# Group norms of a state-space head: token sums and the root's spread moved from TensorE to VectorE's 32x32 transposes and five small transfers

## The chip, the cores and the metric

The kernel runs on one core of a Trainium2 chip. The metric is the device time of one execution in microseconds (us). A core has five engines that work side by side, each through its own list of instructions in a fixed order: TensorE (PE; its weight loads are shown as PEld), VectorE (DVE), ScalarE (ACT), GpSimd (POOL) and SyncE (SP), which here only issues transfers (DMAs). An instruction waits for others by semaphores, and all behind it on its engine wait with it.

## What is computed

One step of a hybrid decoder layer in float32, for 320 tokens: 256 of a prompt and 8 sequences of 8 new ones. The part that matters is the end of the state-space head (SSD). Its output has 2048 columns in four groups of 512; each group has a root-mean-square norm of its own:

```
y = y.reshape(bsz, L, SSM_WIDTH) * jax.nn.silu(z.astype(f32))
yg = y.reshape(bsz, L, SSM_GROUPS, SSM_WIDTH // SSM_GROUPS)
yg = yg * lax.rsqrt(jnp.mean(yg * yg, axis=-1, keepdims=True) + EPS)
y = yg.reshape(bsz, L, SSM_WIDTH) * norm_w.astype(f32)
```

So for every token and group 512 squares are summed, and a root of the mean scales the group. Then `mix = concat(gate_out, y) @ w_out`, a norm and a residual, and a feed-forward part.

## The kernel before, in words

**Layout.** Activations are kept with columns on the 128 partitions and the 320 tokens along the free axis; a group is four blocks of 128x320 (tile `xs`, called y). A sum over a group's columns is therefore one over partitions. Device time goes mostly into products with the weights. Each weight slab of 128x1024 (512 KB) is issued by SP (L118), rounded to a high part on ScalarE (`whi`, L124), and its low part is made on VectorE (`wlo`, L125). Three products (L153 to L155) take the parts with the high and low parts of the activations. Raw, high and low slabs have three buffers each. SP issues a slab when the subtraction three slabs earlier has freed its buffer; ScalarE casts a slab when TensorE has freed the high part three slabs earlier.

**Order.** The program is emitted in a hand-written order: the products of a projection, with small background tasks taken from a list `bg`, one step at each `tick()`, usually one or two per slab. Each engine's list follows from that order and from priorities (`first()` moves things ahead). The SSD of group g (`ssd`) and its norm are such tasks. `heads_out(g, ...)` (L1027) projects z; its evacuation `z_evac` gates y and adds the squares of the four blocks on VectorE to `ssq` (128x320: a partition's sum over four blocks). The task `norm` (L1042) then waits `later` steps (2 or 3), sums and takes the root, waits as many steps, spreads the root, and multiplies and splits y into `ohi`/`olo` (for group 3 into the last blocks of `h_hi`/`h_lo`). These are read by `chunk_out(w_out, 4 + g, ...)` (L1063 to L1080), products `pd` that VectorE adds to `acc_mix` (L249). Between norm and chunk lies the projection of the next group's x (`heads_in_next`), for groups 0 and 1; the chunk of one group overlaps the SSD of the next one.

**The norm.** `token_sums` (L291) has TensorE multiply three slices of `ssq` by a column of ones, giving the 320 sums as three columns over the tokens' partitions. `rsqrt_of` (L258) makes the root on VectorE in eleven small steps on 128x3. `spread` (L300) brings it back to all partitions by three transposes of a broadcast column on TensorE, into PSUM, where the multiplication (L1051) reads it.

**Around it.** In the SSD, cumulative sums come from device memory (`cs<-dacs_d`, L816), become decays on ScalarE (L969, L970) and are masked on VectorE (L972); TensorE reads them for `y_ps` (L983). `xsp` (L842) is the low part of a product operand for `up_ps` (L904). `load_x` (L1110) issues loads of x (`xr`) on SP, used after chunk 7.

Of the kernel before, what the change touches and what calls it, by code (L numbers as in the profile page):

```python
# [9 lines left out]
F32 = mybir.dt.float32  # L10
# [3 lines left out]
ALU = mybir.AluOpType  # L14
# [3 lines left out]
P = 128  # L18
# [3 lines left out]
NT = NP + NS  # L22
# [12 lines left out]
def hybrid_step(  # L35
# [10 lines left out]
    act, dve, pool, pe, sp = nc.scalar, nc.vector, nc.gpsimd, nc.tensor, nc.sync  # L46
# [4 lines left out]
    dr = ctx.enter_context(tc.tile_pool(name="dr", bufs=1, space=DRAM))  # L51
    wp = ctx.enter_context(tc.tile_pool(name="wp", bufs=3))
    tp = ctx.enter_context(tc.tile_pool(name="tp", bufs=2))
# [3 lines left out]
    def misc(name):  # L57
        return ms.tile([P, 512], F32, tag="ms", name=name)
# [41 lines left out]
    def col(i):  # L100
        return prm[:, i:i + 1]


    def first():

        return tc.high_priority(offset=200000)
# [66 lines left out]
    def finish(task):  # L173
        while task in bg:
            tick()
# [79 lines left out]
        pd_last.append(made)  # L255


    def rsqrt_of(ss, scale, n, rows=P):  # L258

        v = tp.tile([P, n], F32, tag=f"rs_v{n}", name="rs_v")[:rows]  # L260
        r = tp.tile([P, n], F32, tag=f"rs_r{n}", name="rs_r", bufs=3)[:rows]
        t = tp.tile([P, n], F32, tag=f"rs_t{n}", name="rs_t")[:rows]
        dve.tensor_scalar(out=v, in0=ss, scalar1=scale, scalar2=EPS, op0=ALU.mult, op1=ALU.add)
        dve.tensor_scalar(out=r.bitcast(I32), in0=v.bitcast(I32), scalar1=-0.5, scalar2=float(0x5F3759DF),
                          op0=ALU.mult, op1=ALU.add)
        for _ in range(3):
            dve.scalar_tensor_tensor(out=t, in0=v, scalar=-0.5, in1=r, op0=ALU.mult, op1=ALU.mult)
            dve.tensor_tensor(out=t, in0=t, in1=r, op=ALU.mult)
            ins = dve.scalar_tensor_tensor(out=r, in0=t, scalar=1.5, in1=r, op0=ALU.add, op1=ALU.mult).ins
        rsqrt_ins.append(ins)  # L270
        return r
# [3 lines left out]
    def rsqrt_by_root(rest, ps, scale, rows=P):  # L275

        v = tp.tile([P, 3], F32, tag="rs_v3", name="rs_v")[:rows]
        r = tp.tile([P, 3], F32, tag="rs_r3", name="rs_r", bufs=3)[:rows]
        t = tp.tile([P, 3], F32, tag="rs_t3", name="rs_t")[:rows]
        s = tp.tile([P, 3], F32, tag="rs_s3", name="rs_s")[:rows]  # L280
        dve.tensor_scalar(out=v, in0=ps if rest is None else rest, scalar1=scale, scalar2=EPS, op0=ALU.mult, op1=ALU.add)
        if rest is not None:
            dve.scalar_tensor_tensor(out=v, in0=ps, scalar=scale, in1=v, op0=ALU.mult, op1=ALU.add)
        rooted.append(act.activation(s, v, AF.Sqrt).ins)
        dve.reciprocal(r, s)
        dve.scalar_tensor_tensor(out=t, in0=v, scalar=-0.5, in1=r, op0=ALU.mult, op1=ALU.mult)
        dve.tensor_tensor(out=t, in0=t, in1=r, op=ALU.mult)
        rsqrt_ins.append(dve.scalar_tensor_tensor(out=r, in0=t, scalar=1.5, in1=r, op0=ALU.add, op1=ALU.mult).ins)
        return r

    def token_sums(*sqs):  # L291

        ps = misc("tsum")
        for c, o in enumerate((0, P, NT - P)):
            for i, sq in enumerate(sqs):
                ins = pe.matmul(ps[:, c:c + 1], sq[:, o:o + P], ones[:, 0:1], start=i == 0, stop=i == len(sqs) - 1).ins  # L296
        sums_ins.append(ins)
        return ps[:, 0:3]

    def spread(r, out=None):  # L300

        ps = misc("spread")
        for c, o in ((2, NT - P), (0, 0), (1, P)):
            spread_ins.append(pe.transpose(ps[:, o:o + P], r[:, c:c + 1].to_broadcast([P, P]), ident).ins)
        if out is not None:
            act.copy(out, ps[:, :NT])
        return ps[:, :NT]

    def add_square(total, x, begins, adder=pool, place=("sq", 2)):
        if begins:  # L310
            act.activation(total, x, AF.Square)
        else:
            sq = tp.tile([P, NT], F32, tag=place[0], name="sq", bufs=place[1])
            act.activation(sq, x, AF.Square)
            adder.tensor_tensor(out=total, in0=total, in1=sq, op=ALU.add)
# [23 lines left out]

    dacs_d = dr.tile([NH, NT + NS], F32, name="dacs_d")  # L340
    tot_d = dr.tile([NH, NB], F32, name="tot_d")


    hp = ctx.enter_context(tc.tile_pool(name="hp", bufs=1))
# [22 lines left out]
    def scaled(ps, func, out):  # L367

        ev = tp.tile([P, NT], F32, tag="pv", name="ev", bufs=4)
        with first():  # L370
            dve.tensor_tensor(out=ev, in0=ps[:, :NT], in1=r1, op=ALU.mult)
        func_ins.append(act.activation(out, ev, func).ins)

    def split(hi, lo, x, scale=None):

        if scale is None:
            act.copy(hi, x)
            made = dve.tensor_tensor(out=lo, in0=x, in1=hi.bitcast(F32), op=ALU.subtract)
        else:
            act.activation(hi, x, AF.Copy, scale=scale)  # L380
            made = dve.scalar_tensor_tensor(out=lo, in0=x, scalar=scale, in1=hi.bitcast(F32), op0=ALU.mult, op1=ALU.subtract)

        return made.ins

    def out_parts(pool_, name):
        return (pool_.tile([P, 4, NT], F32R, tag=f"{name}hi", name=f"{name}hi"),
                pool_.tile([P, 4, NT], F32R, tag=f"{name}lo", name=f"{name}lo"))
# [12 lines left out]
    with ExitStack() as mctx:  # L400
        op = mctx.enter_context(tc.tile_pool(name="op", bufs=1))
# [153 lines left out]
        with tc.tile_pool(name="gp", bufs=1) as gp:  # L555
# [44 lines left out]
            def root():  # L600

                dve.tensor_tensor(out=acc[:, 0, :], in0=acc[:, 0, :], in1=acc[:, 1, :], op=ALU.add)
                ps = misc("tsum")
                for c in range(2):
                    pe.matmul(ps[:, c:c + 1], acc[:, 0, P * c:P * c + P], ones[:, 0:1], start=True, stop=True)
                for h in range(2):
                    pe.matmul(ps[64 * h:64 * h + 64, 2:3], acc[:, 0, NP:NT], ones[:, 0:1], start=True, stop=True, tile_position=(0, 64 * h))
                return rsqrt_of(ps[:, 0:3], 1.0 / D, 3)
# [7 lines left out]
            for n in range(2):  # L616
                ps = banks("ps_v")
                for kt in range(KD):
# [16 lines left out]
                    if n == 0 and kt == 12:  # L635
                        r = root()
# [22 lines left out]
                with first():  # L659
                    for c, g in ((0, 0), (0, 1), (1, 0), (1, 1), (2, 0), (2, 1)):  # L660
                        at, src = slice(0, NS if c == 2 else P), ps[c][g]
                        if c == 2:
# [4 lines left out]
                                                       scale=r[at, c:c + 1]).ins)  # L667
# [4 lines left out]
            def layer_norm():  # L672
# [3 lines left out]
                for c, (o, n) in enumerate(TOK):  # L676
# [3 lines left out]
                    dve.bn_aggr(mv[:n, c, :], st[:n].rearrange("p a b -> p (a b)"))  # L680
                    yield
                lr = rsqrt_of(mv[:, :, 1], 1.0, 3)
                rows = []

# [82 lines left out]
        with tc.tile_pool(name="sd", bufs=1) as sd:  # L767
# [7 lines left out]
            for c in range(4):  # L775
# [6 lines left out]
                else:  # L782
                    b = bsp[:, c - 2]
# [243 lines left out]
            def heads_out(g, rate, later):  # L1027

                ssq = hp.tile([P, NT], F32, tag="ssq", name="ssq")
                y = x_of.pop(g)  # L1030

                def z_evac(j, ps):
                    if j == 0:
                        finish(tasks[g])
                    zs = tp.tile([P, NT], F32, tag="ev", name="zs", bufs=2)
                    with first():
                        scaled(ps, AF.Silu, zs)
                        dve.tensor_tensor(out=y[:, j, :], in0=y[:, j, :], in1=zs, op=ALU.mult)
                        add_square(ssq, y[:, j, :], j == 0, dve)
                project(w_in, Z0 + 512 * g, z_evac, quiet=4, rate=rate)  # L1040

                def norm():  # L1042
                    yield from repeat(None, later)
                    with first():
                        r = rsqrt_of(token_sums(ssq), 1.0 / 512, 3)
                    yield from repeat(None, later)
                    rb = spread(r)

                    res[g] += [h[:, KD - 4:] for h in hT] if g == 3 else out_parts(hp, "o")
                    for j in range(4):  # L1050
                        dve.tensor_tensor(out=y[:, j, :], in0=y[:, j, :], in1=rb, op=ALU.mult)  # L1051
                        split(res[g][0][:, j, :], res[g][1][:, j, :], y[:, j, :], col(prm_at["norm"][3] + 4 * g + j))
                task = norm()
                bg.insert(0, task)
                return task
# [30 lines left out]
            with first():  # L1086
# [8 lines left out]
                r = rsqrt_by_root(most, ps, 1.0 / D)  # L1095
# [48 lines left out]
    with tc.tile_pool(name="fp", bufs=1) as fp:  # L1144
# [149 lines left out]
        r = rsqrt_by_root(most, ps, 1.0 / D)  # L1294
# [7 lines left out]
        for k in BY_POOL:  # L1302
            f = acc[:, k, :]
# [111 lines left out]
```

## Time and profile before

| | |
|---|---|
| median of 3 runs | 1779.38 us (1778.97 to 1780.19) |
| span of the profiled execution | 1779.7 us |
| busy: PE, PEld, VectorE, ScalarE, GpSimd | 99, 96, 66, 46, 15% |
| granted TensorE clock | 0.999 of full |
| moved by DMA | 289.91 MB, 163 GB/s |
| sums of the four groups' squares on TensorE (L296) | 24 records, from 541.8 to 774.8 us |

How to read it: the span runs from the first instruction to the last of one execution with the profiler on, and stands for that execution's own time; it lies 0.3 us above the median of the timed runs and between their ends. Busy shares are averages over stages. A matmul's record is longer than the distance to the next one, since matmuls are pipelined; their starts show the pace. "A <- B: 3.4, 4, 0.9" in a list of waits means that A stood 3.4 us in all for B, 4 times, 0.9 at most. A group row has count, busy us and mean ns, then the idle time just before. A row of DMA issues ends with the median time from issue to landing. In a timeline row stand start, length, engine, line, operation, out<-in, and in brackets the idle time before it and what ended it.

### The profile page before, as it was taken

The numbers are of one execution on the slowest core, as the hardware profiler recorded it, in microseconds if no ns is written. First come the engines' busy times: TensorE is split into PE (matmuls) and PEld (weight loads), VectorE is DVE, ScalarE is ACT, GpSimd is POOL, SyncE is SP. The second block draws the span as 40 slices with busy tenths as digits, with TensorE's granted clock in tenths as the row PEclk, the third lists the DMA queues.
The fourth block names the chain that finished last, engine by engine and source line by source line (L and its number), as shares of the span: only waits on it lengthen the run. The fifth ranks groups of instructions, "written<-read, shape, count | busy, mean of one in ns | idle before, by whom it ended". The sixth has DMA issues, their size and how long they took to land.

```text
span 1779.7 us, 30655 instructions
## 1 busy us (share of the span) xinstructions
PE 1770.5 (99%) x11933; PEld 1715.7 (96%) x11933; DVE 1168.0 (66%) x1999; ACT 819.5 (46%) x1195; POOL 273.5 (15%) x602
## 2 busy tenths in 40 slices
PE   9999999999999999999999999999999999999998
PEld 7789999999999998999999999999999999999998
DVE  7549764656977768677865464756656575656575
ACT  5434555334564547445545333343434343433445
POOL 1202200000331313103121011110102020101004
PEclk9999999999999999999999999999999999999999
DMA  7546645456665665554554545545545545454543
GB/s 260 163 148 177 189 128 154 153 153 188 216 190 190 181 207 168 168 171 145 180 156 146 157 149 151 155 148 152 157 144 156 150 150 155 150 150 155 147 154 107
DMA packets 214417, 289.91 MB, mean 163 GB/s; under 512 B 16384, under 2 KB 143744, under 8 KB 214080
## 3 DMA queue, kind: packets, MB, share of 16 engines
q1 hardware_dynamic: 202544, 268.74, 49.6%
q10 hardware_dynamic: 10016, 14.16, 2.2%
q0 software_dynamic: 1712, 5.05, 1.0%
q8 instruction: 94, 1.54, 0.4%
q14 instruction: 51, 0.42, 0.1%
HBM read 273.08 MB, written 14.82 MB: 162 GB/s over the span
## 4 chain that ended last, share of the span: by engine, by line
PE 97%; DVE 1%; ACT 0%; DMA 0%; issue 0%; POOL 0%; POOLq 0%; ACTq 0%; DVEq 0%
PE ps L153 19%; PE ps L155 19%; PE ps L154 19%; PE pd L153 10%; PE pd L155 10%; PE pd L154 10%; PE ps_v L144 7%; PE y_ps L983 1%; PE up_ps L904 0%; PE yo_ps L887 0%; PE sg L731 0%; PE xt_ps L393 0%; DMA cs<-dacs_d 0%; PE x1p L1278 0%; PE tsum L296 0%
## 5 line engine op out<-in xcount | busy, mean ns | idle before, releaser
L125 DVE TENSOR_TENSOR wlo<-wraw,whi 128x1024 fp32r<-128x1024 f32 (+1 forms) x476 | 582.5, 1224 | 432.4 <-ACT whi L124 430.1
L124 ACT CAST whi<-wraw 128x1024 fp32r<-128x1024 f32 (+1 forms) x475 | 494.8, 1042 | 729.9 <-PE ps L154 392.1
L153 PE MATMUL ps<-h_hi,whi 128*128 128x320 f32 x2268 | 704.0, 311 | 0.0
L154 PE MATMUL ps<-h_lo,whi 128*128 128x320 f32 x2268 | 702.7, 310 | 0.0
L155 PE MATMUL ps<-h_hi,wlo 128*128 128x320 f32 x2268 | 702.2, 310 | 0.0
L153 PEld LDWEIGHTS ps<-h_hi,whi 128*128 128x128 f32 x2268 | 426.2, 188 | 2.6 <-issue 1.6
L154 PEld LDWEIGHTS ps<-h_lo,whi 128*128 128x128 f32 x2268 | 426.3, 188 | 0.7
L155 PEld LDWEIGHTS ps<-h_hi,wlo 128*128 128x128 f32 x2268 | 426.2, 188 | 0.0
L155 PE MATMUL pd<-fhi,wlo 128*128 128x320 f32 x704 | 218.2, 310 | 0.0
L153 PE MATMUL pd<-fhi,whi 128*128 128x320 f32 x704 | 218.2, 310 | 0.0
L154 PE MATMUL pd<-flo,whi 128*128 128x320 f32 x704 | 218.2, 310 | 0.0
L153 PE MATMUL pd<-ohi,whi 128*128 128x320 f32 x448 | 139.4, 311 | 0.0
L155 PE MATMUL pd<-ohi,wlo 128*128 128x320 f32 x448 | 138.7, 310 | 0.0
L154 PE MATMUL pd<-olo,whi 128*128 128x320 f32 x448 | 138.7, 310 | 0.0
L153 PEld LDWEIGHTS pd<-fhi,whi 128*128 128x128 f32 x704 | 132.1, 188 | 0.0
L154 PEld LDWEIGHTS pd<-flo,whi 128*128 128x128 f32 x704 | 132.1, 188 | 0.0
L155 PEld LDWEIGHTS pd<-fhi,wlo 128*128 128x128 f32 x704 | 132.1, 188 | 0.0
L1180 POOL COPY ptf<-pad 128x2 f32<-128x2 f32 x88 | 21.0, 239 | 603.7 <-DVE pad L1168 603.0
L249 DVE TENSOR_TENSOR acc_ffn<-acc_ffn,pd 128x320 f32<-128x320 f32 (+1 forms) x161 | 77.5, 482 | 37.8 <-PE pd L155 36.5
L153 PEld LDWEIGHTS pd<-ohi,whi 128*128 128x128 f32 x448 | 84.1, 188 | 1.4 <-issue 1.0
L154 PEld LDWEIGHTS pd<-olo,whi 128*128 128x128 f32 x448 | 84.1, 188 | 0.3
L155 PEld LDWEIGHTS pd<-ohi,wlo 128*128 128x128 f32 x448 | 84.1, 188 | 0.1
(328 smaller groups left out, 1867.9 us busy)
## 6 DMA issues: line engine op xcount, KB each, us to landing
wraw<-in_ffn_w_up SPq DMA_DIRECT2D x176, 512.0 KB, 3.7
wraw<-in_w_in SPq DMA_DIRECT2D x140, 512.0 KB, 3.8
wraw<-in_ffn_w_down SPq DMA_DIRECT2D x88, 512.0 KB, 3.4
wraw<-in_w_out SPq DMA_DIRECT2D x64, 512.0 KB, 3.4
st<-in_state_ssm SPq DMA_DIRECT2D x32, 256.0 KB, 3.9
out_ssm_state_sample<-st ACTq DMA_DIRECT2D x30, 256.0 KB, 3.4
cs<-dacs_d SPq DMA_DIRECT2D x16, 320.0 KB, 4.7
xr<-in_xT SPq DMA_DIRECT2D x4, 640.0 KB, 4.0
```

The lines of the kernel that those rows point to most:

```text
L124: rounded[:] = [act.copy(hi, raw).ins]
L125: dve.tensor_tensor(out=lo, in0=raw, in1=hi.bitcast(F32), op=ALU.subtract)
L144: made = pe.matmul(out, xi, w[g][wi], start=first and begins, stop=last and ends)
L153: pe.matmul(ps, whi, xhi, start=first, stop=False)
L154: pe.matmul(ps, whi, xlo, start=False, stop=False)
L155: return pe.matmul(ps, wlo, xhi, start=False, stop=last).ins
L249: added_last[:] = [dve.tensor_tensor(out=acc[:, nb, ts], in0=acc[:, nb, ts], in1=ps[:, ts], op=ALU.add).ins]
L983: pe.matmul(ps[64 * i:64 * i + 64, cols], w(hl), x(hl, m, cpx), tile_position=(0, 64 * i), **flags)
L1180: pool.tensor_copy(ptf[:, k, :], pad[:, 256:258])
```

## The change

The sums of the four group norms and the spread of their root no longer use TensorE. `partial_sums` transposes `ssq` in blocks of 32x32 on VectorE, so that a partition holds 32 partitions' values of ten tokens; a sum along the free axis leaves 128x10: for each of four bands of 32 partitions the partial sums of 320 tokens. SP stores these 5 KB to device memory, and four loads (32 partitions each) bring all four bands' sums to every band. `root_by_vector` adds the four, runs `rsqrt_of` on 128x10, and a second transpose, of the root repeated 32 times, writes it to all partitions as `rb` (128x320 in SBUF). The other norms (of the layer's input, output and feed-forward part) stay as they were. The call of `partial_sums` isn't in `first()` any more; the number of steps that `norm` takes from the list is the same. The tiles `turned`, `small` and `rb` share the four buffers `pv` with `ev`.

```diff
-    def rsqrt_of(ss, scale, n, rows=P):
+    def rsqrt_of(ss, scale, n, rows=P, tiles=None):
...
+    SN = NT // 32
+
+    def partial_sums(total, to):
+
+        turned = tp.tile([P, NT], F32, tag="pv", name="turned", bufs=4)
+        dve.transpose(out=turned, in_=total)
+        small = tp.tile([P, NT], F32, tag="pv", name="small", bufs=4)
+        part = small[:, 0:SN]
+        dve.tensor_reduce(out=part, in_=turned.rearrange("p (s f) -> p s f", f=32), axis=mybir.AxisListType.X, op=ALU.add)
+        sp.dma_start(to, part)
+        return small
+
+    def root_by_vector(small, parts, scale, out):
+
+        total, v, r, t = (small[:, SN * i:SN * i + SN] for i in range(1, 5))
+        four = small[:, 5 * SN:9 * SN].rearrange("p (i s) -> p i s", i=4)
+        for q in range(4):
+            sp.dma_start(four[32 * q:32 * q + 32], parts.rearrange("(i t) s -> t i s", i=4))
+        dve.tensor_reduce(out=total, in_=four.rearrange("p i s -> p s i"), axis=mybir.AxisListType.X, op=ALU.add)
+        rsqrt_of(total, scale, SN, tiles=(v, r, t))
+        dve.transpose(out=out.rearrange("p (s f) -> p s f", f=32), in_=r.unsqueeze(2).to_broadcast([P, SN, 32]))
...
+    ssq_d = [dr.tile([P, NT // 32], F32, name=f"ssq_d{i}") for i in range(4)]
...
                 def norm():
                     yield from repeat(None, later)
-                    with first():
-                        r = rsqrt_of(token_sums(ssq), 1.0 / 512, 3)
+                    small = partial_sums(ssq, ssq_d[g])
                     yield from repeat(None, later)
-                    rb = spread(r)
+                    rb = tp.tile([P, NT], F32, tag="pv", name="rb", bufs=4)
+                    root_by_vector(small, ssq_d[g], 1.0 / 512, rb)
```

More of the change, by code (lines that the diff above doesn't have):

```diff
@@ L255, in chunk_out @@
         pd_last.append(made)
-    def rsqrt_of(ss, scale, n, rows=P):
-        v = tp.tile([P, n], F32, tag=f"rs_v{n}", name="rs_v")[:rows]
-        r = tp.tile([P, n], F32, tag=f"rs_r{n}", name="rs_r", bufs=3)[:rows]
-        t = tp.tile([P, n], F32, tag=f"rs_t{n}", name="rs_t")[:rows]
+    def rsqrt_of(ss, scale, n, rows=P, tiles=None):
+        v, r, t = tiles or (tp.tile([P, n], F32, tag=f"rs_{i}{n}", name=f"rs_{i}", bufs=b)[:rows] for i, b in (("v", 2), ("r", 3), ("t", 2)))
         dve.tensor_scalar(out=v, in0=ss, scalar1=scale, scalar2=EPS, op0=ALU.mult, op1=ALU.add)
```

## The prediction

> **What bounds the kernel now.** I read the page first: its span, the busy shares, and the chain that ended last.
>
> ```profile
> span 1779.7 us, 30655 instructions
> PE 1770.5 (99%) x11933; PEld 1715.7 (96%) x11933; DVE 1168.0 (66%) x1999; ACT 819.5 (46%) x1195; POOL 273.5 (15%) x602
> PE 97%; DVE 1%; ACT 0%; DMA 0%; issue 0%; POOL 0%; POOLq 0%; ACTq 0%; DVEq 0%
> ```
>
> TensorE is busy 1770.5 of 1779.7 us and holds 97% of the chain, so an instruction taken from it comes off the end, unless TensorE then waits. The four norms lie between 530 and 800 us. For that stage I asked for the stretches, with wide margins, and for TensorE's own waits. The columns of a stretch are its length, then busy us (and count) of PE, PEld, DVE, ACT and POOL, the clock, the DMA share and GB/s.
>
> ```profile
> 430.00:830.00 400.00, 398.73 (x2882) 377.59 (x2880) 303.62 (x522) 222.35 (x400) 97.59 (x116) 1.00 0.60 186
> 540.00:555.00 15.00, 15.00 (x106) 14.86 (x105) 7.57 (x18) 4.68 (x7) 0.00 (x0) 1.00 0.59 187
> 555.00:570.00 15.00, 15.00 (x106) 14.30 (x105) 14.05 (x28) 9.07 (x16) 3.54 (x11) 1.00 0.39 127
> 655.00:670.00 15.00, 15.00 (x118) 14.80 (x118) 14.04 (x29) 9.07 (x15) 2.62 (x10) 1.00 0.46 153
> 670.00:685.00 15.00, 15.00 (x119) 14.31 (x113) 12.45 (x21) 14.86 (x26) 1.88 (x2) 1.00 0.59 184
> ```
>
> ```profile
> PE up_ps L904 <- DVE xsp L842: 0.8, 2, 0.6
> PE y_ps L983 <- DVE cs L972: 0.2, 1, 0.2
> ```
>
> TensorE is idle only 1.27 us in 400. VectorE is half idle while group 0's sums and root are made (540 to 555) and almost full right after them (14.05 and 14.04 of 15 us): that is where more VectorE work could show. Two kinds of TensorE wait stand in the stage, 1.0 us together, both on VectorE.
>
> **The change part by part.** What TensorE loses, per norm: three products with a column of ones (tsum) and three transposes (spread). The timeline of TensorE around the first sums, and the pieces of the chain for all four (start, length):
>
> ```profile
> 541.46 0.31 PE L155 MATMUL ps<-h_hi,wlo 128*128 128x320 f32 x1
> 541.61 0.31 PE L153 MATMUL ps<-h_hi,whi 128*128 128x320 f32 x1
> 541.79 0.83 PE L296 MATMUL tsum<-ones,ssq 128*128 128x1 f32 x6
> 542.48 0.39 PE L154 MATMUL ps<-h_lo,whi 128*128 128x320 f32 x1
> 542.71 0.30 PE L155 MATMUL ps<-h_hi,wlo 128*128 128x320 f32 x1
> ```
>
> ```profile
> 541.92 0.69 PE tsum L296 x6
> 554.01 0.33 PE spread L304 x3
> 640.65 0.62 PE tsum L296 x6
> 745.12 0.69 PE tsum L296 x6
> 774.23 0.80 PE tsum L296 x6
> 781.59 0.33 PE spread L304 x3
> ```
>
> Matmuls of 320 columns start 0.15 us apart (541.46, 541.61). From 541.61 to 542.71 there are 1.10 us where two steps, 0.29, would do: the sums cost 0.81, that is 0.12 more than the chain's 0.69, since the next matmul's weights come late. With that 0.12 each, the sums are 0.69 + 0.62 + 0.69 + 0.80 + 4 x 0.12 = 3.28 us. The four spreads are 0.33 each (first and last shown), 1.32 us. Together **4.60 us** leave TensorE. In the changed kernel's instruction order just these 24 instructions are gone from TensorE; otherwise it only shifts some small products (y_ps, cb_ps, up_ps) of group 1 by a few places. ScalarE runs two function-table loads fewer there; I count nothing for them.
>
> What VectorE gets, per norm: the eleven steps of the root stay, on 10 columns for 3, and four instructions are new: a transpose of 128x320, a sum over 32 of 128x320, a sum of 4 over 10 columns, and a spreading transpose of 128x320. The trace has no such transposes or sums; the nearest rows:
>
> ```profile
> L315 DVE TENSOR_TENSOR ssq<-ssq,sq 128x320 f32<-128x320 f32 x12 | 5.8, 484 | 0.7 <-ACT sq L314 0.6
> L268 DVE TENSOR_TENSOR rs_t<-rs_t,rs_r 128x3 f32<-128x3 f32 x12 | 1.9, 162 | 0.4
> L125 DVE TENSOR_TENSOR wlo<-wraw,whi 128x1024 fp32r<-128x1024 f32 x95 | 120.6, 1269 | 37.5 <-ACT whi L124 37.2
> DVE rs_v L263 <- PE tsum L296: 3.4, 4, 0.9
> DVE xs L1051 <- PE spread L304: 4.9, 3, 1.7
> ```
>
> Between 0.16 us (three columns) and 1.27 (1024) I take 0.48 for each of the three that pass 320 elements, the row of that size, and 0.2 for the small sum: 1.6 us per norm, with ends at 0.6 and 4.0. On the other side VectorE no longer stands for TensorE's sums and spreads (3.4 and 4.9 us in all, 2.1 per norm). So up to the first multiplication by the root nothing is lost on VectorE; after it the kernel is as before, one instruction placed a little later.
>
> What the queues get, per norm: one store of 128 rows of 40 bytes, and four loads of 128 such rows each, all on SP, where the weight slabs are issued. In the changed order SP runs slab, store, slab, four loads, slab; the store waits for VectorE's sum, the loads wait for the store to land, the slabs behind stand meanwhile. On VectorE the instruction that waits for the loads (the sum of 4) comes two slab subtractions (L125) after the store's sum, in every norm; behind it are queued the next slab's subtraction and the root. Moved along on SP are two loads of x (xr, L1112), a few slabs later; what they bring is used only behind this projection, so they cost nothing.
>
> ```profile
> tot_d<-totc SPq DMA_DIRECT2D x1, 1.0 KB, 2.6
> fst<-in_fconv SPq DMA_DIRECT2D x22, 32.0 KB, 2.9
> cs<-dacs_d SPq DMA_DIRECT2D x16, 320.0 KB, 4.7
> wraw<-in_w_in SPq DMA_DIRECT2D x140, 512.0 KB, 3.8
> 545.78 0.37 SPq L118 DMA_DIRECT2D wraw<-in_w_in  x1
> 544.53 1.23 DVE L125 TENSOR_TENSOR wlo<-wraw,whi 128x1024 fp32r<-128x1024 f32 x1
> 547.99 1.23 DVE L125 TENSOR_TENSOR wlo<-wraw,whi 128x1024 fp32r<-128x1024 f32 x1 [2.16 <-ACT whi L124]
> 553.90 1.05 ACT L124 CAST whi<-wraw 128x1024 fp32r<-128x1024 f32 x1 [2.47 <-PE ps L154]
> 555.18 1.22 DVE L125 TENSOR_TENSOR wlo<-wraw,whi 128x1024 fp32r<-128x1024 f32 x1
> ```
>
> The store of a small tile to device memory landed in 2.6 us; small loads take 2.9 (fst), loads from such scratch 4.7 (cs). From the sum: 2.6, then four issues of 0.37 = 1.5, then 2.9 to 4.7, so 7.0 to 8.8 us. VectorE gets there two subtractions later, and they come 3.5 us apart (544.53, 547.99): 7 us. It stands 0 to 1.8 us. I take 1 us, in a stretch where it was half idle.
>
> What hides this. The slab issued at 545.78, when the subtraction of 544.53 had ended, fills the buffer that is cast three slabs later, at 553.90: it lands at 549.6 and has 4.3 us to spare. Store and loads keep SP for at most 2.6 + 1.5 = 4.1 us, and part of that SP stands for the next subtraction anyway. The cast itself waits for TensorE to free a buffer, so two slabs of 3.5 us are still ahead of it: TensorE wants the new one at 560.9, and the subtraction ends at 556.4. VectorE may be 4.5 us late before TensorE notices; it is 1 to 2 late. Without this cover each us late would cost one, four times over.
>
> Where it is tight. The next use of the normalized group:
>
> ```profile
> 560.48 1.01 DVE L381 SCALAR_TENSOR_TENSOR olo<-xs,prm,ohi 128x320 fp32r<-128x320 f32 x2
> 564.74 0.31 PE L153 MATMUL pd<-ohi,whi 128*128 128x320 f32 x1
> 799.56 0.49 DVE L249 TENSOR_TENSOR acc_mix<-acc_mix,pd 128x320 f32<-128x320 f32 x1 [0.96 <-PE pd L155]
> 800.82 0.31 PE L154 MATMUL pd<-h_lo,whi 128*128 128x320 f32 x1
> ```
>
> Group 0 had 3.2 us to spare (561.5 to 564.74). For group 3 the changed order puts the last low part right behind the addition that began at 799.56; at some 0.5 us each it is there at 800.5, and TensorE wants it at 800.82: 0.3 to spare, a few tenths lost at worst. The masked decays of groups 1 and 2 (L972) follow the full stretches after a norm, and TensorE already waited 0.2 us for one, so there a late VectorE goes straight to TensorE. The bounds are 0 (the 2.55 idle us of 670 to 685 absorb it) and a norm's whole 1.6 at each of two places, 3.2. I take 0.4, near the row: 0.2 again for either group.
>
> **The sum.** 4.6 off, 0.4 back: 4.2 us. The profiled span is 1779.7 and the median 1779.4 (runs 1779.0 to 1780.2), so span and time may be taken as one, and 1779.4 - 4.2 = **1775.2 us**. About 0.2%, 3.6 us, is what a measurement of this kernel can tell from no change.
>
> **The rivals.**
> (a) VectorE gives the gain back. The 1.6 us are added ahead of stretches that are 94% full and reach TensorE as waits on L972. For it: the row with 0.2 us shows no slack there. Against: the freed 2.1 us, and the idle time of 670 to 685. Two places at 1.6: 1779.4 - 4.6 + 3.2 = 1778.0; all four norms, 1781.2. No change within 0.2%.
> (b) Slower: the loads land late. VectorE stands at the sum of 4, the slab subtraction behind it comes too late, TensorE runs dry. It decides from a stand of more than 4.5 us, so loads that land 11.5 us after the sum, not 7.0 to 8.8. To end 3.6 us above today it must eat 8.2 us, 2.05 in each norm: landing at 13.6 us, and 1783.0 us. For it: 640 short rows per norm behind half-megabyte slabs in one queue. Against: every small row above.
> (c) TensorE's time isn't freed, since its waits only move: the earlier TensorE comes, the longer it stands at L842 and L972. At most the gain of the first two norms is lost, 0.81 + 0.33 and 0.74 + 0.33, 2.2 us: 1777.0.
> (d) Short rows land in twice the time. Then the loads come 2 x 2.6 + 1.5 + 2 x 2.9 = 12.5 us after the sum, 1.0 us past the 11.5 of (b), in each norm: 1775.2 + 4 = 1779.2. Against it stands that rows of 32 bytes landed in 2.6 us where the half megabyte of a slab took 3.8.
> The Trainium skill ("DMA: Bandwidth & Descriptors", Specifications) says that below 512 bytes a transfer pays a read-modify-write; this speaks against the change, and (d) is what it would do here. The 2.6 us show no doubling.
>
> **How the numbers follow.** Forecast 0.62, (a) 0.21, (c) 0.04, (d) 0.03, (b) 0.10. Faster by over 0.2% is the forecast alone, 0.62; (a), (c) and (d) make no difference, 0.28; slower is (b), 0.10. Low end: 4.6 and today's two waits of 1.0 gone as well, and 0.4 for the spread of the runs: 1773.4. High end: (a) at 1778.0 and 1 us of (b)'s kind: 1779.0. That leaves out most of (b) and the far part of (a).
>
> **What would show it.** Right: TensorE's row lists 36 fewer products (six for each norm's sums, three for its spread) with no wait on L125's or L124's results; the two transposes near 0.5 us; the sum of 4 waiting under 2 us; the casts (L124) not waiting for slab loads. Wrong: a TensorE wait named whi, wlo or ohi (then (b), or the norm itself is late), or waits at L983 and L904 above 2 us together (then (a) or (c)).

## The result and the profile after

The changed kernel took 1775.21 us (median of 15 runs, 1773.91 to 1778.89), the kernel before beside it 1779.66 (15 runs, 1778.44 to 1782.19). The ratio is 0.9976, interval 0.9969 to 0.9983: 4.4 us or 0.24% faster, and 0.0 us from the forecast of 1775.2. So close a hit is luck, as the terms show below.

The page of the changed kernel: span, busy shares, and the chain that ended last.

```profile
span 1773.0 us, 30633 instructions
PE 1765.1 (100%) x11897; PEld 1711.9 (97%) x11897; DVE 1173.7 (66%) x2015; ACT 817.9 (46%) x1193; POOL 274.5 (15%) x602
PE 98%; DVE 1%; issue 0%; ACT 0%; ACTq 0%; DVEq 0%
```

TensorE has 36 products fewer (11933 to 11897) and still holds the chain. The same stretches of the stage, and TensorE's waits there:

```profile
430.00:830.00 400.00, 398.80 (x2870) 377.13 (x2869) 313.12 (x549) 222.98 (x402) 99.69 (x116) 1.00 0.60 187
540.00:555.00 15.00, 15.00 (x104) 15.00 (x103) 9.82 (x24) 5.58 (x7) 0.00 (x0) 1.00 0.53 155
555.00:570.00 15.00, 15.00 (x106) 14.30 (x105) 13.42 (x27) 9.38 (x16) 5.75 (x14) 1.00 0.49 162
655.00:670.00 15.00, 15.00 (x124) 14.74 (x123) 14.90 (x31) 11.01 (x19) 4.02 (x11) 1.00 0.60 187
670.00:685.00 15.00, 14.96 (x111) 13.11 (x110) 11.19 (x20) 12.81 (x31) 4.14 (x4) 1.00 0.58 172
```

```profile
PE up_ps L925 <- DVE xsp L863: 0.5, 2, 0.2
```

VectorE has taken 9.5 us more work into the stage (303.62 to 313.12), some of it where it stood half idle (7.57 to 9.82 of 15 us). The row of TensorE's wait for the masks (`y_ps` on `cs`, 0.2) is gone, and its wait for `xsp` fell from 0.8 to 0.5. Lines of the new kernel stand 21 higher behind L360: the masks are L993, the multiplication by the root L1072.

The way of group 0 through VectorE and SP:

```profile
539.05 0.51 DVE L312 STREAM_TRANSPOSE turned<-ssq 128x320 f32<-128x320 f32 x1
539.60 0.49 DVE L315 TENSOR_REDUCE small<-turned 128x10 f32<-128x320 f32 x1
546.94 0.23 DVE L325 TENSOR_REDUCE small<-small 128x10 f32<-128x40 f32 x1 [1.24 <-DMA small<-ssq_d]
550.93 0.51 DVE L327 STREAM_TRANSPOSE rb<-small 128x320 f32<-128x320 f32 x1
```

```profile
540.12 0.34 SPq L316 DMA_DIRECT2D ssq_d<-small  x1
542.79 1.77 SPq L324 DMA_DIRECT2D small<-ssq_d  x4
```

```profile
small<-ssq_d SPq DMA_DIRECT2D x16, 5.0 KB, 3.0
ssq_d<-small SPq DMA_DIRECT2D x4, 5.0 KB, 2.6
```

The sum ends at 540.09, SP issues the store at once and the loads when it has landed, and 6.85 us after the sum VectorE goes on. It had come 1.24 us too early.

**Where the time came from.** The two profiled spans differ by 6.7 us (1779.7 and 1773.0), the medians by 4.4. To split this I take three stretches of TensorE: up to the first product of the first `fin_ps` (ahead of all four norms), from there to the first product of the stage behind them ("the stretch" from here on), and the rest. In before, then in the changed kernel:

```profile
505.79 1.02 PE L1011 MATMUL fin_ps<-xde,btok 128*128 128x512 f32 x2
833.26 0.86 PE L190 MATMUL ps<-h_hi,whi 128*128 128x320 f32 x4 [0.16 <-ACT h_hi L380]
```

```profile
503.08 1.02 PE L1032 MATMUL fin_ps<-xde,btok 128*128 128x512 f32 x2
825.34 0.85 PE L190 MATMUL ps<-h_hi,whi 128*128 128x320 f32 x4 [0.16 <-ACT h_hi L401]
```

The stretch with the norms fell from 327.47 to 322.26: **5.21 us** are the change's. (The expectations below were written with 327.3 and 322.1, read a little coarser.) Ahead of it 2.71 us lie, in code that the change doesn't touch. They arise at one place of the execution of before, where TensorE stands for `later_s` and then runs slowly:

```profile
245.02 0.41 PE L546 MATMUL dec_ps<-sp_e,later_s 64*128 64x32 f32 x2 [0.34 <-POOL later_s L544]
246.46 0.41 PE L546 MATMUL dec_ps<-sp_e,later_s 64*128 64x32 f32 x2 [0.69 <-POOL later_s L544]
247.23 0.47 PE L153 MATMUL ps<-h_hi,whi 128*128 128x320 f32 x1
247.49 0.47 PE L154 MATMUL ps<-h_lo,whi 128*128 128x320 f32 x1
```

```profile
248.00:250.00 2.00, 2.00 (x9) 2.00 (x9) 0.00 (x0) 0.00 (x0) 0.00 (x0) 0.50 0.54 202
```

It stood 1.03 us, and then its products started 0.26 us apart instead of 0.15, at a granted clock of 0.50, for some 3.5 us. The last 16 us of the changed kernel had such a slow piece too (0.50 at 1760 to 1762) and gave 1.2 us back: 2.7 + 5.2 - 1.2 = 6.7. Neither is an effect of the change, as its second profile shows (below).

### The profile page after: what moved, and what is told of

It reads as the page before. It is cut to its first block, busy times and chain, and to the rows that moved or that the text cites. A ratio compares the mean times of both kernels' runs of the same rounds, so it can differ in the third digit from the quotient of the medians.

```text
span 1773.0 us, 30633 instructions
## 1 busy us (share of the span) xinstructions
PE 1765.1 (100%) x11897; PEld 1711.9 (97%) x11897; DVE 1173.7 (66%) x2015; ACT 817.9 (46%) x1193; POOL 274.5 (15%) x602
## 4 chain that ended last, share of the span: by engine, by line
PE 98%; DVE 1%; issue 0%; ACT 0%; ACTq 0%; DVEq 0%
PE ps L153 19%; PE ps L154 19%; PE ps L155 19%; PE pd L153 10%; PE pd L155 10%; PE pd L154 10%; PE ps_v L144 7%; PE y_ps L1004 1%; PE up_ps L925 0%; PE sg L752 0%; PE yo_ps L908 0%; PE xt_ps L414 0%; PE early L70 0%; PE x1p L1299 0%; DVE xsp L863 0%
```

## The experiments

All times are medians, with those of the kernel before on the same chip beside them; the stretch is that of the one profiled execution (327.47 for the kernel before, which has one profile only).

| kernel | stretch, us | time, us | before beside it | ratio |
|---|---|---|---|---|
| changed | 322.26 | 1775.21 | 1779.66 | 0.9976 (0.9969 to 0.9983) |
| after_again | 322.66 | 1775.57 | 1779.67 | 0.9977 (0.9967 to 0.9986) |
| sums_back | 326.54 | 1778.44 | 1779.62 | 0.9994 (0.9985 to 1.0003) |
| spreads_back | 323.67 | 1776.50 | 1779.62 | 0.9982 (0.9973 to 0.9991) |
| no_transfers | 323.15 | 1775.71 | 1779.62 | 0.9981 (0.9972 to 0.9990) |
| vector_twice | 322.76 | 1774.80 | 1779.19 | 0.9978 (0.9968 to 0.9987) |
| halves | 327.40 | 1776.89 | 1779.67 | 0.9987 (0.9977 to 0.9996) |
| pairs | 338.12 | 1789.74 | 1779.39 | 1.0058 (1.0037 to 1.0079) |
| single_elements | 359.43 | 1814.49 | 1779.19 | 1.0198 (1.0183 to 1.0213) |
| two_trips | 338.02 | 1791.33 | 1779.62 | 1.0064 (1.0052 to 1.0077) |
| two_trips_root_first | 332.40 | 1782.99 | 1779.19 | 1.0019 (1.0010 to 1.0028) |
| first_norm_too | 322.11 | 1774.38 | 1779.19 | 0.9970 (0.9960 to 0.9981) |

**TensorE's two parts, given back one at a time.**

```diff
+                    with first():
+                        token_sums(ssq)
                     small = partial_sums(ssq, ssq_d[g])
```

> The changed kernel with the three products with a column of ones (tsum) issued again in each norm, their result read by nobody; VectorE's way stays. Measured on TensorE from the first product of the first fin_ps to the first product of the root mean square's own stage (ps with the new h_hi): 327.3 us before, 322.1 after. Theory (the gain is TensorE's own time): plus 3.3 us, to 325.4, and about 1778.5 us in all. Rival (a part of the gain came from VectorE no longer standing for TensorE's sums, and here it doesn't stand for them): plus 2 us or less, to at most 324.1.

The stretch grew by 4.28 us, the time by 3.2. Followed product by product against the changed kernel, the four sums cost 0.80, 0.73, 0.81 and 1.03 us, together 3.37, the 3.3 of the theory; the rival's limit of 2 us is passed by far. The other 0.9 is a stand of TensorE at a `y_ps` product. First two rows of the changed kernel, then three of this one:

```profile
581.90 0.42 ACT L983 ACTIVATE cpx<-cs 128x256 f32<-128x256 f32 x1 [0.60 <-DMA cs<-dacs_d]
585.66 0.89 DVE L993 TENSOR_TENSOR cs<-cs,cb_cms 128x320 f32<-128x320 f32 x2
```

```profile
583.59 0.42 ACT L983 ACTIVATE cpx<-cs 128x256 f32<-128x256 f32 x1 [1.49 <-DMA cs<-dacs_d]
587.34 0.89 DVE L993 TENSOR_TENSOR cs<-cs,cb_cms 128x320 f32<-128x320 f32 x2
587.93 0.90 PE L1004 MATMUL y_ps<-cs,xdt 128*64 128x128 f32 x7 [0.91 <-PE y_ps L1004]
```

The profile puts the wait down to an earlier product, but that had long ended; the product begins 0.1 us after the first mask of L993 ends (587.82), here and in `spreads_back`, `vector_twice`, `halves` and `pairs`, where it waits as well. The mask was late because the load of the cumulative sums took 5.38 us to land, against 4.49 in the changed kernel, and ScalarE and VectorE waited behind it. In the thirteen profiles this load takes 4.2 to 5.4 us; why isn't shown.

```diff
                     yield from repeat(None, later)
+                    spread(ones)
                     rb = tp.tile([P, NT], F32, tag="pv", name="rb", bufs=4)
```

> The changed kernel with the three spreading transposes issued again on TensorE in each norm, of a tile of ones, their result read by nobody. Theory: plus 1.3 us in the same stretch of TensorE, 322.1 to 323.4, and about 1776.5 us in all. Rival (VectorE's stand for the spread was the cost, not the three products): no change, 322.1. If both kernels together give back less than 5.2 us, the rest of the gain is not TensorE's products.

Plus 1.41 in the stretch, plus 1.3 in time: the theory's numbers (1.3 and 1776.5). Product by product the four spreads cost 0.33 us each, 1.33 together. That the whole stretch agrees too is partly luck: 0.75 us more were lost at the same masks, whose load landed in 5.32 us, and 0.68 were gained between the second spread and the third, where the scheduler laid group 1's products in another order. The gain is TensorE's own instructions.

**Are the transfers hidden?**

```diff
-        sp.dma_start(to, part)
...
-        four = small[:, 5 * SN:9 * SN].rearrange("p (i s) -> p i s", i=4)
-        for q in range(4):
-            sp.dma_start(four[32 * q:32 * q + 32], parts.rearrange("(i t) s -> t i s", i=4))
+        four = small[:, 0:SN].unsqueeze(2).to_broadcast([P, SN, 4])
```

> The changed kernel without the store and the four loads: each quarter of the partitions keeps its own sum, taken four times, so the sum over the four quarters is left out. Theory (the transfers are hidden wholly): the stretch of TensorE stays within 0.3 us of 322.1, though VectorE's waits at the sum of 4 (3.2 us in all) go. Rival (b, in small: the standing of VectorE reaches TensorE): 1 to 3 us shorter.

This kernel leaves out the exchange between the bands, so its roots are those of a quarter of the columns. The stretch was 0.9 us longer without the transfers (0.5 longer than in the second execution of the changed kernel, below), over the 0.3 allowed but on the other side of the rival; the time doesn't differ (1775.71). The scheduler that lays out each engine's list gave TensorE before's order again here, less the 24 instructions and with one product elsewhere, and TensorE's waits are before's to the tenth: `up_ps` 0.8 and `y_ps` 0.2. So the five transfers per norm cost nothing that shows; about 0.5 of the 0.9 us lie where the order of group 1's small products is another in the changed kernel. Against before, 327.47 - 323.15 = 4.32 us: product by product the sums and spreads are again 4.7 of it, and 0.4 were lost in between, with nearly the same order, which is how far two executions differ.

**VectorE's work doubled.**

```diff
-        dve.transpose(out=turned, in_=total)
+        for _ in range(2):
+            dve.transpose(out=turned, in_=total)
```

and so for the sum over 32 and for the spreading transpose.

> The changed kernel with each norm's three long VectorE instructions (both transposes and the sum over 32) done twice, 1.5 us more of VectorE per norm; TensorE's instructions and their order are the same. Theory (VectorE has room): the stretch of TensorE from the first fin_ps to the stage of the next root mean square stays within 0.4 us of 322.3, about 1775.4 us in all. Rival (a: VectorE's time reaches TensorE in the full stretches behind a norm): 1.5 us at two places or more, stretch 325.3 to 328.

322.76, and 1774.80 us in all. The time shows no loss; the stretch is 0.5 us above the changed kernel's, a little over the 0.4 allowed, and 0.1 above that of its second execution. TensorE's order is the changed kernel's, and all of the 0.5 lies at the masks of L993 (the product of 587 us). The way there is VectorE's: a slab subtraction ended at 577.98, SP issued the slab that it freed at 578.01 and only then the load of the cumulative sums (578.44), 0.5 us later against TensorE's products than in the changed kernel. So rival (a) as I had priced it (1.6 us at each of two places) is refuted, but its place is right: a late VectorE reaches TensorE at the masks. (VectorE's order behind the norm is another here, so how much of the 0.5 is the doubled work itself isn't shown.)

**How late may the loads land?** Four kernels make them later. In the first the parts go through memory twice.

```diff
-        sp.dma_start(to, part)
+        sp.dma_start(to[0], part)
+        hop = small[:, 9 * SN:10 * SN]
+        sp.dma_start(hop, to[0])
+        sp.dma_start(to[1], hop)
```

> The changed kernel with a second way through device memory: the stored sums are loaded into one tile and stored again, all on SP, before the four loads. The loads should land some 13.5 us after the sum, not 6.9. Theory by the prediction's cover (VectorE may be 4.5 us late, which is 11.5 us after the sum): TensorE waits about 2 us in each norm on the slabs' results, 8 us in all, stretch near 330, time near 1783. Rival (the cover is larger than worked out, since a late VectorE also has the next slab's buffers in hand): stretch within 1 us of 322.1.

The stretch was 15.8 us longer: worse than the theory, and by another way. TensorE's longest waits:

```profile
PE pd L153 <- ACT ohi L404: 5.7, 2, 4.1
PE y_ps L1007 <- DVE st L930: 2.1, 1, 2.1
PE pd L153 <- ACT h_hi L404: 1.5, 1, 1.5
```

The first and the last are for the normalized group itself, the middle one is for a state; none is for a slab. VectorE stood only 0.7 us in group 0, but from the sum of 4 (553.57) to `rb` (565.79) it took 12.2 us, where the changed kernel took 4.0: the scheduler had put the next group's convolution between the root's steps. So the next kernel puts the root first:

```diff
+        with first():
             rsqrt_of(total, scale, SN, tiles=(v, r, t))
             dve.transpose(out=out.rearrange("p (s f) -> p s f", f=32), ...)
```

> The kernel with two trips through memory (stretch 338.0, TensorE waiting 7.2 us for ohi and h_hi), with the steps of the root and the spreading transpose put first in VectorE's order, ahead of the convolution of the next group. The loads land as late as there. Theory (it was VectorE's order that made the norm late, not the landing: there the root took 12.2 us from the sum of 4 to rb, in the changed kernel 4.5): most of the 15.8 us come back, stretch 324 to 328, no wait on ohi in group 0. Rival (the landing itself is too late): stretch 334 or more.

332.40: 5.6 of the 15.8 us came back, between the two numbers. `rb` began 5.3 us after the sum of 4, yet TensorE still waited 2.5 us for `xsp`, 1.8 for `olo` and 0.9 for `ohi`. Order and landing both count here, and the kernel can't part them, because the scheduler answers a late landing with another order. The next three keep the changed kernel's order on every engine and only cut the stored rows into pieces of 4, 8 and 20 bytes:

```diff
-    ssq_d = [dr.tile([P, NT // 32], F32, name=f"ssq_d{i}") for i in range(4)]
+    ssq_d = [dr.tile([NT // 32, P], F32, name=f"ssq_d{i}") for i in range(4)]
...
-        sp.dma_start(to, part)
+        sp.dma_start(to.rearrange("s p -> p s"), part)
```

with loads to match; `pairs` and `halves` store as (5, 128, 2) and (2, 128, 5).

> The changed kernel with the parts stored turned, so that the store and the four loads move single elements of 4 bytes instead of rows of 40; the order on every engine is the same. Theory: the store and loads take longer, but as long as they land within 10 us of the sum (VectorE 4.5 us late) the stretch stays within 0.5 us of 322.3. If short pieces cost twice the time each (12.5 us after the sum), VectorE stands 6 us, some 1.5 us over the cover, and the stretch grows by 1 to 2 us a norm, to 326 to 330. Rival to the cover: any stand of VectorE over 2 us shows, as the stretches behind the norms are full: stretch 330 or more already at 10 us.

The store landed in 10.6 us, and VectorE's stand in the first norm, with TensorE's answer and its clock, looks like this:

```profile
558.96 0.20 DVE L325 TENSOR_REDUCE small<-small 128x10 f32<-128x40 f32 x1 [11.42 <-DMA small<-ssq_d]
```

```profile
560.78 0.64 PE L155 MATMUL ps<-h_hi,wlo 128*128 128x320 f32 x1 [4.63 <-DVE wlo L125]
```

```profile
562.00:564.00 2.00, 2.00 (x9) 2.00 (x9) 1.86 (x6) 0.45 (x1) 0.00 (x0) 0.50 0.70 243
```

This is rival (b) as the prediction told it: VectorE stands at the sum of 4, the slab's subtraction behind it is late, TensorE runs dry. It waited 15.0 us for `wlo` in three norms. In the first, 11.42 - 4.63 = 6.8 us of the stand were free of that wait, where the prediction had 4.5 (an estimate, as are the free stands below: the stand less TensorE's answer).

> As single_elements, but the store and the loads move pairs of elements, 8 bytes; the order on every engine is the same as in the changed kernel. From the store of rows (2.6 us for 128 pieces) and of single elements (10.6 us for 1280) the store of 640 pieces should land in 6.2 us, an estimate on a straight line, and the loads 10.5 to 11.5 us after the sum, so VectorE stands 4.5 to 6 us in each norm. Theory by single_elements (VectorE stood 11.4 us in the first norm and TensorE then waited 4.6, so 6.7 us are free): TensorE waits nothing, stretch within 1 us of 322.3. Theory by the prediction's cover (4.5 us): up to 1.5 us of waiting in a norm and slow products behind it, stretch 325 to 332.

Both theories failed: 338.12. There is hardly a slab among the waits (0.4 us for `wlo`), so the slabs' cover is indeed over 4.5 us; but TensorE lost 15.9 us elsewhere, most of it at the masks (L993, 2.9 us), at `xdt` (L938, 2.5), at `h_hi` of group 3 (2.0), at a product held up by the root's steps (L265, 1.8) and in two pieces of 3.4 us at a clock of 0.50, some 1.5 each.

> As pairs, but with pieces of five elements, 20 bytes (256 pieces in the store); the order on every engine is the changed kernel's. On the line through the stores measured (rows 2.6, pairs 6.7, single elements 10.6 us) the store should land in 3.4 us, the loads some 8 us after the sum, and VectorE should stand about 2 us in each norm, where it stood 0.8 with rows and 5.4 with pairs. In vector_twice, 1.5 us more on VectorE cost 0.5 in the stretch; in pairs, 4.6 us more of standing cost 15.9. Theory (the cover ends between them, at the masked decays): 1.2 us more of standing is still nearly free, stretch 322.3 to 323.5. Rival (every us of standing costs TensorE in proportion, 0.86 us for each): 4 x 1.2 x 0.86 = 4 us, stretch 326.

The profiled execution, the longest of ten, has 327.40, near the rival. The median is 1.3 us above that of the changed kernel on the same chip, so a usual execution lies between the two numbers. VectorE's stands and TensorE's answers in groups 0 and 1:

```profile
550.03 0.22 DVE L325 TENSOR_REDUCE small<-small 128x10 f32<-128x40 f32 x1 [3.63 <-DMA small<-ssq_d]
651.51 0.22 DVE L325 TENSOR_REDUCE small<-small 128x10 f32<-128x40 f32 x1 [3.79 <-DMA small<-ssq_d]
```

```profile
579.36 0.78 PE L1004 MATMUL y_ps<-cs,xdt 128*64 128x64 f32 x12 [1.48 <-DVE xdt L938]
681.68 0.54 PE L1004 MATMUL y_ps<-cs,xdt 128*64 128x128 f32 x5 [1.68 <-DVE cs L993]
```

So the stand that is free is 3.63 - 1.48 = 2.15 and 3.79 - 1.68 = 2.11 us. In `pairs` group 0 stood 4.84 and TensorE waited 2.46 at the same product: 2.4 are free. The changed kernel stands 1.24 and 1.25. **So its loads may land some 0.9 us later in groups 0 and 1 before TensorE waits.** That holds for this order of VectorE's instructions: in `vector_twice`, where the order behind the norm is another, VectorE stood 3.29 us in group 0 and TensorE lost only the 0.5. In the third norm of `halves` a stand of 1.75 cost nothing.

**The changed kernel once more.**

> The changed kernel once more, unchanged. The profiled execution of before stood 1.0 us for later_s near 245 us and then ran at a lower clock, 2.7 us in all; that of the changed kernel lost 1.2 us in its last 16 us. If both are chance, this execution has its first fin_ps between 503.1 and 503.7 (or at 505.8), its stretch is 322.3 within 0.2, and its tail is 16.0 or 17.2 us.

The first `fin_ps` came at 503.99, 0.3 us beyond the band, after a wait of 0.2 for an addition and some products that started late; the stretch was 322.66, 0.2 over its band; the tail was 1.0 us shorter, without the slow piece. So the stretch of one execution is good to 0.4 us. Of the thirteen profiled executions the stall for `later_s` stands in two, before and single_elements: chance, not the change.

**A version that goes further.**

```diff
-                    if n == 0 and kt == 12:
-                        r = root()
+                    if n == 0 and kt == 10:
+                        small = root()
+                    if n == 0 and kt == 14:
+                        r = root_columns(small)
...
-                        spread(r, r1)
```

with `root()` ending in `partial_sums`, and `root_columns` in `root_by_vector` and four copies for the columns that ScalarE needs.

> The changed kernel with the norm of the input (root of x, in the first 80 us) made in the same way: sums by VectorE begun two slabs earlier, the root's spread by VectorE, its three columns by four small copies; TensorE loses four sums products and three transposes there, worth 0.9 us (0.6 and 0.33). Theory (hidden like the others): the first fin_ps comes 0.9 us earlier, at 502.2 to 502.6 instead of 503.1 to 503.5, and the time is 0.9 us below the changed kernel's. Rival (the first 80 us are nearer to the transfers' limit, and the store and loads hold SP ahead of slabs): TensorE waits there and fin_ps comes 1 us or more later.

```profile
502.25 1.02 PE L1037 MATMUL fin_ps<-xde,btok 128*128 128x512 f32 x2
```

The first `fin_ps` stands 0.8 us ahead of the changed kernel's, as expected; the time is 1774.38, 0.83 below, but the kernel before is 0.47 faster on that chip as well. It has the lowest median here; by the timed runs alone (0.9970 against 0.9976, intervals overlapping) it isn't told from the changed one.

## Why the prediction was right

The signs that it named for being right are there: 36 products fewer, no wait on `whi` or `wlo` in the stage, 0.5 us of waits at `up_ps` and none listed at the masks (the limit was 2 together), a sum of 4 that waits 1.25 us at most, and no cast in the stage that waits for a slab's load. Rival (c) is out by the same row, since the waits that it let grow became shorter.

**TensorE loses 4.60 us.** Right, and 0.1 too small. Followed to the second product behind each, the changed kernel's products come earlier by 0.80, 0.73, 0.80 and 1.03 at the four sums (3.36, where the prediction had 3.28) and by 0.33 at each spread (1.32): 4.7 us. The 0.12 us added to each sum for late weights was 0.11 in three groups and 0.23 in the last. `sums_back` and `spreads_back` give the same 3.37 and 1.33 back.

**The masked decays take 0.4 back.** The step that failed: nothing was lost on balance. The stretch fell by 5.21 us, in the second execution by 4.81, which is 0.5 and 0.1 more than left TensorE. Between 655 and 745 us 0.42 and 0.45 were gained in the two executions; there the scheduler laid group 1's last `y_ps` products earlier than before. `no_transfers`, with the old order on TensorE, lost 0.13 there and has the old waits, although VectorE doesn't stand for TensorE's sums there either. So that gain is luck of the order, not VectorE's freed time. The rest (0.12 gained, in the second execution 0.33 lost, at 590 to 640 us) is within what two executions differ by. The mechanism isn't idle, though: `vector_twice` pays 0.5 us by it.

**VectorE's 1.6 us.** 0.51 + 0.49 + 0.23 + 0.51 = 1.74; the row of 128x320 was the right neighbour. **Landing 7.0 to 8.8 us after the sum, a stand of 1 us.** 6.85, 7.85, 6.82 and 8.14 in the four groups; 3.2 us of standing in four norms, 0.8 each.

**Group 3 has 0.3 us to spare.** Its last low part and the product that reads it:

```profile
792.12 0.55 DVE L402 SCALAR_TENSOR_TENSOR h_lo<-xs,prm,h_hi 128x320 fp32r<-128x320 f32 x1
```

```profile
792.89 0.31 PE L154 MATMUL pd<-h_lo,whi 128*128 128x320 f32 x1
```

Ready at 792.67, read at 792.89: 0.2 to spare, and no wait.

**The cover of 4.5 us, and (b) deciding at 11.5 us.** Right in its mechanism, wrong as the bound. The slab path holds longer than said (6.8 us). But ahead of it the masks and `xdt` run out, at a stand of 2.1 to 2.4 us, some 0.9 us behind today's landing. The prediction had named that place as tight and priced a late VectorE there by its work alone. (a) and (b) are one danger: a stand at the sum of 4 comes out at the masks. **(d)** didn't happen; 12.5 us after the sum would have cost far more than the 4 us that it was priced at, since `pairs`, whose loads landed 10.3 us after it in group 0, lost 15.9.

**The base.** The prediction, like the table ahead of it, took span and time as one. They differ by 1.7 us (1773.0 and 1774.69 for one execution), so by this estimate the profiled execution of before took 1781.4, about 2 us more than its median, for which the 2.7 us at 245 us are enough; the forecast was safe from this only because it went out from the median.

The sum of the terms as measured is 4.7 + 0.1 to 0.5 = 4.8 to 5.2 us, inside the interval of the timed gain (0.9969 to 0.9983, 3.0 to 5.5 us); the medians themselves give 4.4 and, the second time, 4.1, and the stretch of before rests on one execution. The forecast had 4.2: a freed time 0.1 too small and a loss that wasn't there. The hit to 0.0 us needed a second error besides: the base of three runs, 1779.38, was 0.3 below the median of fifteen, which made up for a gain that was 0.25 larger than forecast.

## What to carry to other kernels

Where one engine holds 97% of the chain, an instruction taken from it is worth its own length, however roundabout the way by which another engine does it, as long as that way's result isn't due. What bounds it is the first deadline of all that is queued behind the waiting instruction, so list those deadlines one by one, not only the best known. And compare two kernels between marks on the bounding engine, not by spans: here the spans said 6.7, the marks 5.2, and product by product 4.7 was the change's own.

## What the runs showed of the hardware

**A short wait can cost more than itself.** After TensorE had stood 1.03 us (before, 245 us) or 1.68 us (`halves`, 681 us), its products started 0.26 us apart instead of 0.15 for 3 us or more, at a granted clock of 0.50: the 1.03 us came to 2.7. The Trainium skill ("TensorE: Matmul & The Clock Gate", Part 1: The HAM clock gate) has the clock at half after an idle window of about 3.4 us and full again after about 3.4 us of work. The return agrees (the slow pieces last 3.4 us here); the fall came here after idle pieces of 0.34 and 0.69 us. Not every such wait brings it: after 1.48 us (`halves`, 579 us) and 2.46 us (`pairs`, 580 us) the clock stayed at 1.00. No run here shows what decides.

**A store's landing goes with its pieces, a load's doesn't.** The stores of rows, halves, pairs and single elements, 5 KB each (128, 256, 640 and 1280 pieces):

```profile
ssq_d<-small SPq DMA_DIRECT2D x4, 5.0 KB, 4.1
```

```profile
ssq_d<-small SPq DMA_DIRECT2D x4, 5.0 KB, 6.7
```

```profile
ssq_d<-small SPq DMA_DIRECT2D x4, 5.0 KB, 10.6
small<-ssq_d SPq DMA_DIRECT2D x16, 5.0 KB, 3.3
```

With the 2.6 us of rows that is (10.6 - 2.6) / 1152 = 7 ns for each further piece over the whole range, and 12 ns over the first 128; the loads went from 3.0 to 3.3 (3.5 in pairs). All of these lie under the 512 bytes of the Trainium skill's rule ("DMA: Bandwidth & Descriptors", Specifications), which the prediction cites; no doubling stood at 40 bytes, and what decided was into how many pieces a store of 5 KB was cut (number and length of the pieces go together here).
